# Layer ends of a two-network kernel: scaling shared by ScalarE and VectorE, weight splits behind the norm chains, transposes among the last products

## The chip, the cores and the metric

The kernel runs on one core of one Trainium2 chip. The metric is the device time of one execution in microseconds (us). The engines are named as in the profile: PE is TensorE's products (PEld its weight loads), ACT is ScalarE, DVE is VectorE, POOL is GpSimd and SP is SyncE, which issues the weight transfers.

## The reference

One sequence of 256 tokens with 1024 channels, all in float32, goes through five layers, one after another.

1. Stick-breaking attention with 16 heads: `h = h + rmsnorm(merge_heads(o) @ sb_w_o, sb_post_g)`.
2. A gated feed-forward net with a causal convolution of width 3 (`w_up` to 2 x 2816 channels, `w_down` back): `h = h + rmsnorm(f, ffn_post_g)`.
3. Forgetting attention: keys, values and gates from `rmsnorm(h, kv_norm_g) @ w_kvf`, queries from `rmsnorm(h, fox_pre_g) @ fox_w_q`, again added to h behind a norm.
4. The second feed-forward net.
5. A pooling layer (`x + y @ pool_w_out`, no norm behind it), and then a latent attention layer (`mla_*`), which starts with `rmsnorm_2(x, mla_norm) @ mla_w_in`, and a last norm.

Every layer starts with a norm of h, and every norm needs whole rows of h:

```python
def rmsnorm(x, g):
    xf = x.astype(jnp.float32)
    y = xf * lax.rsqrt(jnp.mean(xf * xf, axis=-1, keepdims=True) + RMS_EPS)
    return (y * g.astype(jnp.float32)).astype(x.dtype)
```

## The kernel before, in words

**Three products for one.** Every float32 operand x is kept as a high part (x rounded to fp32r by a copy on ACT, `hi_copy`, line 64) and a low part (x minus the high part, on DVE, `lo_sub`, line 68). A product of two such operands is three products on TensorE: high by high, high by low, low by high (`mm3`, `mm3s`). So whatever TensorE reads must first pass ACT (high) and then DVE (low).

**Weights.** All weights of the kernel form one list of chunks (1 MB each, mostly), and each chunk is cut into parts of up to 128 x 1024 elements. There are three buffers for raw chunks and eight for high and low parts (`wh`, `wl`). `bg_hi` copies the next part of the list on ACT, if the part eight places before it has been used up in the program. `bg_lo` does the DVE subtraction of every part that has its high half and not yet its low half, and, behind the last part of a chunk, issues on SP the load of the chunk three places on. `bg(m)` does m parts of both. `get_w` and `get_rows` return a function that hands out slices of a part; if the part isn't split by then, it is split at that place in the program.

**Order.** The whole program is under a manual schedule: each engine executes its instructions in the order in which the Python code emits them. An instruction that waits holds up all that were emitted behind it on its engine.

**Token blocks.** The 256 tokens are two blocks (i = 0 and 1) of 128 partitions. The residual h lies with tokens on partitions. A layer's input is the scaled h, transposed by TensorE in eight 128 x 128 squares per block (`transpose_split`: four transposes into one PSUM bank, then a high copy on ACT and a low subtraction on DVE; `all_T` does this twice, for channels 0 to 511 and 512 to 1023). [...]

**Layer ends.** `edge` (line 478) writes the end of a layer and the start of the next. `tail0` and `tail1` are the last products of blocks 0 and 1, each into two accumulators of 512 channels. `add` is either `post_add` (squares on ACT, product with the gain on DVE, rstd on POOL, then h on DVE, line 402) or, behind pooling, `plain_add` (line 409). `norm_r` squares both halves of h on ACT (line 383), does the pending weight splits (`bg_lo`) and lets POOL compute rstd (lines 346 to 349). `scaled` (line 370) multiplies h by rstd and gain, in two halves on DVE. Block 0's end runs beside block 1's last products; block 1's end runs beside the next layer's first products on block 0. Five places call `edge`: the two attentions (through `attention`, line 534), the two feed-forward nets (line 789) and pooling (line 1087).

**What follows a layer end.** Behind an attention `ffn` starts with `nat_start` (line 433): for block 0 and then block 1, two weight chunks (c) in two halves (k) give four quarters of 12 products, each with one weight part; the `hook`, which transposes block 1, stands between the blocks. Behind the second feed-forward net pooling starts with the same `nat_start`. Behind the first one `values_all` (line 452) runs over two column halves n of the value weights, and within each over the two blocks i, with hooks at given places (n, i, k). Behind pooling the latents are computed by `lat_a` (24 products with four parts) and `lat_b` (line 1129).

Of the kernel before, what the change touches and what calls it, by code (L numbers as in the profile page):

```python
# [15 lines left out]
P = 128  # L16
S = 256
NT = S // P
D = 1024
# [17 lines left out]
def tile_net(ctx: ExitStack, tc: tile.TileContext, t, out):  # L37
# [54 lines left out]
    def acc_tile(name):  # L92
        return pacc.tile([P, 512], F32, tag="acc", name=name)
# [7 lines left out]
    def tok(i):  # L101
        return slice(i * P, (i + 1) * P)
# [79 lines left out]
    def bg_lo():  # L182
        while nxt["lo"] < nxt["hi"]:
            n = nxt["lo"]
            q = parts[n]
            lo_sub(q["wl"], q.pop("raw"), q["wh"], q["scale"])
            nxt["lo"] += 1
            if n == specs[q["chunk"]][1][-1]:
                load_w(q["chunk"] + RAWB)
# [105 lines left out]
    def get_rows(idx, n=2):  # L295

        at = [get_w(i) for i in idx]
        return lambda k, c0, m: at[k // n](k % n, c0, m)
# [37 lines left out]
    def mean_sq(srcs, n):  # L336

        ss = sm.tile([P, 2], F32, tag="ss", name="ss")
        for j, x in enumerate(srcs):
            square(x, n, ss[:, j:j + 1])  # L340
        return ss[:, 0:len(srcs)]
# [29 lines left out]
                                     op0=ALU.mult, op1=ALU.mult)  # L371
        return a

    def norm_r(i):

        ss = mean_sq([h[:, i, s_] for s_ in HALF], D)
        bg_lo()
        return rstd_of(ss, "rn")

    def square(x, n, ss):  # L380

        junk = jk.tile([P, 512], BF16, tag="junk", name="junk")
# [47 lines left out]
            mm3(acc[n], at(oT, ko, tok(i)), w(kw, n * 512, 512), first and j == 0,  # L430
                last and j == len(ks) - 1)

    def nat_start(aT, views, hook):

        w = [get_w(v) for v in views]
        res = []
        for i in range(NT):
            acc = acc_tile("accS")
            for c in range(2):
                for k in range(0, KD, 4):  # L440
                    ks = range(k, k + 4)
                    mm3s(acc[:, c * 256:(c + 1) * 256], [at(aT, x, tok(i)) for x in ks],
                         [w[c](x, 0, 256) for x in ks], k == 0, k == 4)
            if i == 0:
                hook()
            x = nat.tile([P, D], F32, tag="a", name="xs")
            act.activation(out=x[:, 0:512], in_=acc, func=AF.Copy)
            res.append(x)
            bg(4)
        return res  # L450

    def values_all(xT, views, vv, hooks):


        for n in range(2):
            w = get_rows(views[n], 4)
            for i in range(NT):
                acc = acc_tile("accV")
                for k in range(0, KD, 2):
                    if (n, i, k) in hooks:  # L460
                        hooks[n, i, k]()
                    ks = range(k, k + 2)
                    mm3s(acc, [at(xT, x, tok(i)) for x in ks], [w(x, 0, 512) for x in ks],
                         k == 0, k == 6)
                    if n or i:
                        bg(1)
                if (n, i, KD) in hooks:
                    hooks[n, i, KD]()
                split(vv[0][:, i, HALF[n]], vv[1][:, i, HALF[n]], acc)
                if n == i == 0:  # L470
                    bg(2)

    def nat_T(ps, xs, c):

        for i in range(NT):
            pe.transpose(ps[:, tok(i)], xs[i][:, tok(c)], ident)

    def edge(tail0, tail1, acc, add, g, dst):


        tail0()
        half, fin = add(0, acc[0])
        half(0)
        half(1)
        bg_hi()
        fin()
        r0 = norm_r(0)
        tail1()
        half, fin = add(1, acc[1])
        half(0)  # L490
        a0 = scaled(0, r0, g)
        half(1)
        all_T(a0, dst, 0)
        bg_hi()
        fin()
        r1 = norm_r(1)
        return scaled(1, r1, g), (r0, r1)

    def attention(s0, s1, s2, s3, post, w_ids, oT, g_post, dst, hook, late, acc0_tile):

# [6 lines left out]
        for p in range(1, KD - 1):  # L507
# [6 lines left out]
            if p == 3:  # L514
# [16 lines left out]
        s3(KD - 1)  # L531
        out_rows(acc1, 1, oT, wo, K8[3:4], False, False)
        bg(1)
        return edge(lambda: out_rows(acc0, 0, oT, wo, K8[7:8], False, True),
                    lambda: out_rows(acc1, 1, oT, wo, K8[4:8], False, True, by_half=True),
                    (acc0, acc1), lambda i, a: post_add(i, a, g_post), g_next, dst)[0]

    def heads_out(p, vv, pr, oT):

# [189 lines left out]
    def ffn(l, aT, a1, late, dst):  # L729
# [3 lines left out]
        with tc.tile_pool(name=f"ff{l}", bufs=3) as ff, tc.tile_pool(name=f"fg{l}", bufs=1) as fg:  # L733
# [23 lines left out]
                split(gT[0][:, f, :], gT[1][:, f, :], y[:, 1, :])  # L757
                bg(1)

            xs = nat_start(aT, [W["up_g", l, 0], W["up_u", l, 0]], lambda: all_T(a1, aT, 1))  # L760
            for c in range(1, NF // 2):
                wg, wu = get_w(W["up_g", l, c]), get_w(W["up_u", l, c])
                for pp in range(2):
# [15 lines left out]
            for m, f in enumerate(DOWN):  # L779
# [5 lines left out]
                if m < NF - TAIL[0]:  # L785
# [1 line left out]
            tail = [[(f, f) for f in DOWN[NF - x:]] for x in TAIL]  # L787
            w = lambda f, c0, n: wd[f // 2](f % 2, c0, n)
            return edge(lambda: out_rows(acc[0], 0, gT, w, tail[0], False, True, by_half=True),
                        lambda: out_rows(acc[1], 1, gT, w, tail[1], False, True, by_half=True),  # L790
                        acc, lambda i, a: post_add(i, a, g_post), g, dst)


    def causal_mask(m):
# [43 lines left out]
    with tc.tile_pool(name="fxa", bufs=1) as fxa:  # L838
# [7 lines left out]
        with tc.tile_pool(name="fx", bufs=2) as fx, tc.tile_pool(name="fxv", bufs=1) as fxv:  # L846
# [8 lines left out]
            def scale_a(i):  # L855
                af[i] = scaled(i, rn[i], g_a)

            values_all(sT, W["fx_v"], vv, {
                (0, 0, KD): lambda: all_T(a1, sT, 1),
                (0, 1, 0): lambda: scale_a(0), (0, 1, 4): lambda: scale_a(1),  # L860
                (1, 0, 0): lambda: all_T(af[0], fT, 0),
                (1, 1, 0): lambda: all_T(af[1], fT, 1)})
            g_post = gain("fox_post_g", 0)


# [86 lines left out]
    with tc.tile_pool(name="pl", bufs=2) as pl_, tc.tile_pool(name="plc", bufs=1) as plc:  # L952
# [126 lines left out]
        def lat_mm(x, i, k0, k1):  # L1079
            n, w = lat_w[x]  # L1080
            if k0 == 0:
# [3 lines left out]
                 k0 == 0, k1 == KD)  # L1085

        a1 = edge(lambda: out_rows(acc[0], 0, st["y", 3], wo, k4, False, True, by_half=True),
                  lambda: out_rows(acc[1], 1, st["y", 3], wo, k4, False, True, by_half=True),
                  acc, plain_add, g_pre, mT)[0]
        aT = mT  # L1090


# [408 lines left out]
```

## Time and profile before

| | |
|---|---|
| median of 3 runs | 981.46 us (980.86 to 981.47) |
| profiled execution | 981.37 us, of which the span 979.7 us |
| mean granted TensorE clock | 0.999 |
| busy PE, DVE, ACT, POOL | 965.0, 756.7, 609.7, 71.9 us |
| chain that ended last | PE 88%, ACT 5%, DVE 3%, POOL 2% |

The rows that follow in the prediction are of four kinds. A timeline row has the start in us, the busy time in us, the engine, the line, the operation, the tiles written and read, their shapes, a count where like instructions are merged, and in brackets the idle time before it and the instruction that ended it. A row of a stretch has its bounds, its length, and the engine's busy time in it with the number of instructions, then the granted clock and the DMA share. A row that counts copies of weight parts ("wh<-raw") has their number since the start, the shortest, mean and longest in ns, and the first and the last start in us. The page's first row has each engine's busy time and share of the span.

### The profile page before, as it was taken

The numbers are of one execution on the slowest core, as the hardware profiler recorded it, in microseconds if no ns is written. First come the engines' busy times: TensorE is split into PE (matmuls) and PEld (weight loads), VectorE is DVE, ScalarE is ACT, GpSimd is POOL, SyncE is SP. The second block draws the span as 40 slices with busy tenths as digits, with TensorE's granted clock in tenths as the row PEclk, the third lists the DMA queues.
The fourth block names the chain that finished last, engine by engine and source line by source line (L and its number), as shares of the span: only waits on it lengthen the run. The fifth ranks groups of instructions, "written<-read, shape, count | busy, mean of one in ns | idle before, by whom it ended". The sixth has DMA issues, their size and how long they took to land.

```text
span 979.7 us, 17580 instructions
## 1 busy us (share of the span) xinstructions
PE 965.0 (99%) x6954; PEld 893.3 (91%) x6954; DVE 756.7 (77%) x1302; ACT 609.7 (62%) x1049; POOL 71.9 (7%) x181
## 2 busy tenths in 40 slices
PE   8999999999999999999999999999999999999997
PEld 6999789999888899889999988899999899999996
DVE  7577788999955969977999973776868677887876
ACT  7499866767744657666676753665434555766563
POOL 1022220000002000020000000200000020110100
PEclk9999999999999999999999999999999999999999
DMA  8724346675572744435666575375555344644521
GB/s 304 241 91 147 130 156 207 198 234 197 179 253 86 230 160 151 157 102 173 202 228 205 183 256 174 100 246 206 175 201 194 110 135 136 212 157 140 163 95 43
DMA packets 116164, 170.27 MB, mean 174 GB/s; under 512 B 4218, under 2 KB 93682, under 8 KB 116082
## 3 DMA queue, kind: packets, MB, share of 16 engines
q1 hardware_dynamic: 116002, 169.15, 51.8%
q8 instruction: 54, 0.88, 0.4%
q14 instruction: 28, 0.23, 0.1%
q0 software_dynamic: 64, 0.00, 0.0%
q10 hardware_dynamic: 16, 0.00, 0.0%
HBM read 168.10 MB, written 1.05 MB: 173 GB/s over the span
## 4 chain that ended last, share of the span: by engine, by line
PE 88%; ACT 5%; DVE 3%; POOL 2%; issue 1%; DMA 1%; SPq 0%; POOLq 0%; DVEq 0%; ACTq 0%
PE psu L79 10%; PE psu L80 10%; PE psu L81 10%; PE accD L81 4%; PE accD L80 4%; PE accD L79 4%; PE psq L79 3%; PE psq L81 3%; PE psq L80 3%; PE accO L79 2%; PE accO L81 2%; PE accO L80 2%; PE accP L79 1%; PE accP L81 1%; PE accP L80 1%; DVE wl L68 1%
## 5 line engine op out<-in xcount | busy, mean ns | idle before, releaser
L68 DVE TENSOR_TENSOR wl<-raw,wh 128x1024 fp32r<-128x1024 f32 (+3 forms) x300 | 352.6, 1197 | 88.5 <-ACT wh L64 85.5
L64 ACT ACTIVATE wh<-raw 128x1024 fp32r<-128x1024 f32 (+3 forms) x316 | 315.4, 1026 | 77.9 <-PE accD L81 30.3
L79 PE MATMUL psu<-aT,wh 128*128 128x256 f32 x864 | 239.5, 277 | 0.0
L80 PE MATMUL psu<-aT,wh 128*128 128x256 f32 x864 | 239.2, 277 | 0.0
L81 PE MATMUL psu<-aT,wl 128*128 128x256 f32 x864 | 239.2, 277 | 0.0
L79 PEld LDWEIGHTS psu<-aT,wh 128*128 128x128 f32 x864 | 162.2, 188 | 0.2
L81 PEld LDWEIGHTS psu<-aT,wl 128*128 128x128 f32 x864 | 162.2, 188 | 0.0
L80 PEld LDWEIGHTS psu<-aT,wh 128*128 128x128 f32 x864 | 162.0, 188 | 0.0
L748 DVE SCALAR_TENSOR_TENSOR yc<-psu,conv,yc 128x255 f32<-128x255 f32 (+1 forms) x160 | 73.5, 480 | 11.6 <-ACT yc L741 8.6
L79 PE MATMUL accD<-wh,gh 128*128 128x512 f32 x176 | 68.7, 390 | 0.0
L81 PE MATMUL accD<-wh,gl 128*128 128x512 f32 x176 | 68.5, 389 | 0.0
L80 PE MATMUL accD<-wl,gh 128*128 128x512 f32 x176 | 68.5, 389 | 0.0
L346 POOL TENSOR_TENSOR ss<-ss,epsc 128x1 f32<-128x1 f32 x23 | 11.6, 506 | 612.3 <-ACT junk L383 612.3
L79 PE MATMUL psq<-aT,wh 128*128 128x256 f32 x192 | 54.0, 281 | 0.1
L80 PE MATMUL psq<-aT,wh 128*128 128x256 f32 x192 | 53.4, 278 | 0.0
L81 PE MATMUL psq<-aT,wl 128*128 128x256 f32 x192 | 53.4, 278 | 0.0
L741 ACT ACTIVATE yc<-psu,conv 128x256 f32<-128x256 f32 x80 | 40.8, 560 | 19.8 <-PE psu L81 19.8
L753 ACT ACTIVATE yc<-yc 128x256 f32<-128x256 f32 x44 | 18.4, 418 | 48.5 <-DVE yc L748 48.5
L64 ACT ACTIVATE qkh<-psq 128x512 fp32r<-128x512 f32 x32 | 19.0, 594 | 33.5 <-PE psq L81 33.3
L80 PEld LDWEIGHTS accD<-wl,gh 128*128 128x128 f32 x176 | 33.1, 188 | 6.8
L79 PEld LDWEIGHTS accD<-wh,gh 128*128 128x128 f32 x176 | 33.0, 188 | 6.8
L81 PEld LDWEIGHTS accD<-wh,gl 128*128 128x128 f32 x176 | 33.0, 188 | 6.8
(347 smaller groups left out, 2272.7 us busy)
## 6 DMA issues: line engine op xcount, KB each, us to landing
raw<-in_w_up_dram SPq DMA_DIRECT2D x44, 1024.0 KB, 5.0
raw<-in_w_down_dram SPq DMA_DIRECT2D x22, 1024.0 KB, 5.9
raw<-in_pool_w_in_dram SPq DMA_DIRECT2D x16, 1024.0 KB, 7.0
raw<-in_sb_w_qkv_dram SPq DMA_DIRECT2D x10, 1024.0 KB, 5.3
raw<-in_w_kvf_dram SPq DMA_DIRECT2D x8, 1024.0 KB, 5.6
raw<-in_pool_w_out_dram SPq DMA_DIRECT2D x8, 1024.0 KB, 5.0
raw<-in_mla_w_in_dram SPq DMA_DIRECT2D x8, 1024.0 KB, 5.3
raw<-in_mla_w_out_dram SPq DMA_DIRECT2D x8, 1024.0 KB, 5.6
```

What stands on the lines that cost most here:

```text
L64: act.activation(out=hi, in_=src, func=AF.Copy, scale=scale)
L68: (eng or dve).tensor_tensor(out=lo, in0=src, in1=hi.bitcast(F32), op=ALU.subtract)
L79: pe.matmul(ps, lhsT=l[0], rhs=r[0], start=first, stop=False)
L80: pe.matmul(ps, lhsT=l[0], rhs=r[1], start=False, stop=False)
L81: pe.matmul(ps, lhsT=l[1], rhs=r[0], start=False, stop=last)
L346: pool.tensor_tensor(out=s0, in0=s0, in1=epsc[:, 0:1], op=ALU.add)
L741: act.activation(out=y[:, u, :], in_=ps[:, u * S:(u + 1) * S], func=AF.Identity, bias=cp[:, 132 + q:133 + q], scale=cp[:, 88 + q:89 + q])
L748: dve.scalar_tensor_tensor(out=y[:, u, d:S], in0=ps[:, u * S:(u + 1) * S - d], scalar=w, in1=y[:, u, d:S], op0=ALU.mult, op1=ALU.add)
L753: act.activation(out=y[:, 0, :], in_=y[:, 0, :], func=AF.Gelu_apprx_tanh)
```

## The change

- `norm_r` is gone. `norm_1` squares h, multiplies the second half of h by the gain on DVE, and computes rstd; `norm_2` multiplies that half by rstd on ACT and does the first half (h times rstd times gain) on DVE. The pending weight splits come once at the end of `edge`, and with a `tail2` also ahead of block 0's transposes.
- The feed-forward nets and pooling split block 1's last products (`halves`): all but the last step of the second accumulator ahead of block 0's transposes, that step (three products) behind them.
- The attentions have no `tail2` and lose the second `bg_hi`; the update of h stands between the two evacuations of block 0's transposes. Their `tail0` does the four products with the high half of oT first and the two with the low half last.
- In `ffn`, the hook of `nat_start` comes before the last quarter of block 0.
- `values_all` behind the first feed-forward net does block 0 for both column halves and then block 1; the hooks move accordingly.

```diff
-    def norm_r(i):
-
-        ss = mean_sq([h[:, i, s_] for s_ in HALF], D)
-        bg_lo()
-        return rstd_of(ss, "rn")
...
-    def nat_start(aT, views, hook):
+    def nat_start(aT, views, hook, early=False):
...
                 for k in range(0, KD, 4):
+                    if early and (i, c, k) == (0, 1, 4):
+                        hook()
                     ks = range(k, k + 4)
...
-            if i == 0:
+            if i == 0 and not early:
                 hook()
...
+    def values_all(xT, views, vv, hooks, order=((0, 0), (0, 1), (1, 0), (1, 1))):
+        w = [get_rows(views[n], 4) for n in range(2)]
+        for n, i in order:
+            acc = acc_tile("accV")
...
+    def norm_1(i, g):
+
+        ss = mean_sq([h[:, i, s_] for s_ in HALF], D)
+        a = nat.tile([P, D], F32, tag="a", name="a")
+        dve.tensor_tensor(out=a[:, HALF[1]], in0=h[:, i, HALF[1]], in1=g[:, HALF[1]], op=ALU.mult)
+        return a, rstd_of(ss, "rn")
+
+    def norm_2(i, a, r, g):
+
+        act.activation(out=a[:, HALF[1]], in_=a[:, HALF[1]], func=AF.Copy, scale=r)
+        dve.scalar_tensor_tensor(out=a[:, HALF[0]], in0=h[:, i, HALF[0]], scalar=r,
+                                 in1=g[:, HALF[0]], op0=ALU.mult, op1=ALU.mult)
+
+    def edge(tail0, tail1, tail2, acc, add, g, dst):
...
         fin()
-        r0 = norm_r(0)
+        a0, r0 = norm_1(0, g)
         tail1()
         half, fin = add(1, acc[1])
         half(0)
-        a0 = scaled(0, r0, g)
-        half(1)
-        all_T(a0, dst, 0)
-        bg_hi()
-        fin()
-        r1 = norm_r(1)
-        return scaled(1, r1, g), (r0, r1)
+        norm_2(0, a0, r0, g)
+        if tail2:
+            bg_lo()
+            all_T(a0, dst, 0)
+            tail2()
+            half(1)
+            bg_hi()
+            fin()
+        else:
+            half(1)
+            transpose_split(a0, dst[0], 0, 0)
+            fin()
+            transpose_split(a0, dst[1], 0, 4)
+        a1, r1 = norm_1(1, g)
+        norm_2(1, a1, r1, g)
+        bg_lo()
+        return a1, (r0, r1)
+
+    def halves(acc, i, oT, w, ks):
+        def run(n, js):
+            for j in js:
+                ko, kw = ks[j]
+                mm3(acc[n], at(oT, ko, tok(i)), w(kw, n * 512, 512), False, j == len(ks) - 1)
+
+        m = len(ks)
+        return lambda: (run(0, range(m)), run(1, range(m - 1))), lambda: run(1, [m - 1])
...
-        return edge(lambda: out_rows(acc0, 0, oT, wo, K8[7:8], False, True),
+
+        def tail0():
+            xh, xl = at(oT, KD - 1, tok(0))
+            w = [wo(KD - 1, 512 * n, 512) for n in range(2)]
+            for n in range(2):
+                for y in w[n]:
+                    pe.matmul(acc0[n], lhsT=xh, rhs=y, start=False, stop=False)
+            for n in range(2):
+                pe.matmul(acc0[n], lhsT=xl, rhs=w[n][0], start=False, stop=True)
+
+        return edge(tail0,
                     lambda: out_rows(acc1, 1, oT, wo, K8[4:8], False, True, by_half=True),
-                    (acc0, acc1), lambda i, a: post_add(i, a, g_post), g_next, dst)[0]
+                    None, (acc0, acc1), lambda i, a: post_add(i, a, g_post), g_next, dst)[0]
...
-            xs = nat_start(aT, [W["up_g", l, 0], W["up_u", l, 0]], lambda: all_T(a1, aT, 1))
+            xs = nat_start(aT, [W["up_g", l, 0], W["up_u", l, 0]], lambda: all_T(a1, aT, 1), True)
...
-                        lambda: out_rows(acc[1], 1, gT, w, tail[1], False, True, by_half=True),
-                        acc, lambda i, a: post_add(i, a, g_post), g, dst)
+                        *halves(acc[1], 1, gT, w, tail[1]), acc, lambda i, a: post_add(i, a, g_post), g, dst)
...
             values_all(sT, W["fx_v"], vv, {
-                (0, 0, KD): lambda: all_T(a1, sT, 1),
+                (1, 0, 2): lambda: all_T(a1, sT, 1),
                 (0, 1, 0): lambda: scale_a(0), (0, 1, 4): lambda: scale_a(1),
-                (1, 0, 0): lambda: all_T(af[0], fT, 0),
-                (1, 1, 0): lambda: all_T(af[1], fT, 1)})
+                (1, 1, 0): lambda: all_T(af[0], fT, 0),
+                (1, 1, 6): lambda: all_T(af[1], fT, 1)},
+                ((0, 0), (1, 0), (0, 1), (1, 1)))
...
-                  lambda: out_rows(acc[1], 1, st["y", 3], wo, k4, False, True, by_half=True),
-                  acc, plain_add, g_pre, mT)[0]
+                  *halves(acc[1], 1, st["y", 3], wo, k4), acc, plain_add, g_pre, mT)[0]
```

More of the change, by code (lines that the diff above doesn't have):

```diff
@@ L450, in nat_start @@
         return res
[L452 to L471, printed above, removed]
+    def values_all(xT, views, vv, hooks, order=((0, 0), (0, 1), (1, 0), (1, 1))):
+        w = [get_rows(views[n], 4) for n in range(2)]
+        for n, i in order:
+            acc = acc_tile("accV")
+            for k in range(0, KD, 2):
+                if (n, i, k) in hooks:
+                    hooks[n, i, k]()
+                ks = range(k, k + 2)
+                mm3s(acc, [at(xT, x, tok(i)) for x in ks], [w[n](x, 0, 512) for x in ks],
+                     k == 0, k == 6)
+                if n or i:
+                    bg(1)
+            if (n, i, KD) in hooks:
+                hooks[n, i, KD]()
+            split(vv[0][:, i, HALF[n]], vv[1][:, i, HALF[n]], acc)
+            if n == i == 0:
+                bg(2)
     def nat_T(ps, xs, c):
@@ L476, in nat_T @@
             pe.transpose(ps[:, tok(i)], xs[i][:, tok(c)], ident)
-    def edge(tail0, tail1, acc, add, g, dst):
+    def norm_1(i, g):
[8 more added lines that the diff above has]
+    def edge(tail0, tail1, tail2, acc, add, g, dst):
         tail0()
```

## The prediction, as it was put on record before the run

> **What bounds the kernel now.** I read the page first (busy shares), then TensorE's waits, then the busy time of the stretches around the five layer ends, then the order of instructions there, and last how many weight parts ScalarE had copied by given times.
>
> ```profile
> PE 965.0 (99%) x6954; PEld 893.3 (91%) x6954; DVE 756.7 (77%) x1302; ACT 609.7 (62%) x1049; POOL 71.9 (7%) x181
> ...
> 127.29:129.53 2.24, 1.43 (x10) 1.00 0.00 0
> 135.09:136.45 1.36, 1.33 (x10) 1.00 1.07 377
> 311.57:313.06 1.49, 1.04 (x10) 1.00 0.00 0
> 318.75:320.09 1.34, 1.17 (x9) 1.00 0.73 269
> 433.90:436.12 2.22, 1.41 (x9) 1.00 0.89 275
> 441.69:443.12 1.43, 1.37 (x11) 1.00 0.00 0
> 618.24:619.73 1.49, 1.04 (x10) 1.00 0.00 0
> 625.29:626.76 1.47, 1.41 (x11) 1.00 0.87 246
> 779.06:780.35 1.29, 1.04 (x9) 1.00 0.04 13
> 785.94:786.73 0.79, 0.79 (x11) 1.00 0.00 0
> ```
>
> TensorE is busy 965.0 of 979.7 us, so only its gaps can be won. Each stretch above runs from the slot after the last product ahead of a set of eight transposes to the first product behind it. The last needs 0.79 us: eight transposes that wait for nothing. The other nine take 14.33 us, 7.2 us more than nine times 0.79. That is all that layer ends can give.
>
> What the change may break is the order of DVE and ACT, which execute their instructions as written:
>
> ```profile
> L64 ACT ACTIVATE wh<-raw x39: 615/1044/1064, 6.7 to 122.7; 128x1024 fp32r<-128x1024 f32 x31, 128x512 fp32r<-128x512 f32 x8
> ...
> L64 ACT ACTIVATE wh<-raw x40: 615/1044/1064, 6.7 to 130.0; 128x1024 fp32r<-128x1024 f32 x32, 128x512 fp32r<-128x512 f32 x8
> ...
> 125.11 1.22 DVE L68 TENSOR_TENSOR wl<-raw,wh 128x1024 fp32r<-128x1024 f32 x1
> 125.42 0.95 POOL L346 TENSOR_TENSOR ss<-ss,epsc 128x1 f32<-128x1 f32 x1 [1.69 <-ACT junk L383]
> 127.31 1.42 DVE L370 SCALAR_TENSOR_TENSOR a<-h,rstd,g 128x512 f32<-128x512 f32 x2 [0.39 <-POOL rstd L349]
> 128.88 1.26 ACT L64 ACTIVATE aT<-psT 128x512 fp32r<-128x512 f32 x2 [0.45 <-PE psT L356]
> 130.78 1.40 DVE L402 SCALAR_TENSOR_TENSOR h<-y,rstd,h 128x512 f32<-128x512 f32 x2
> 132.10 1.22 DVE L68 TENSOR_TENSOR wl<-raw,wh 128x1024 fp32r<-128x1024 f32 x1
> 134.30 1.42 DVE L370 SCALAR_TENSOR_TENSOR a<-h,rstd,g 128x512 f32<-128x512 f32 x2 [0.98 <-POOL rstd L349]
> ```
>
> Counting the parts that the code defines (12 for the values, 16 for q and k, 8 for the output weights), the first part of w_up is number 37. So the copy at 122.7 is w_up part 3 of the stage that starts at 129.53, and the copy at 130.0 is part 4. That stage (nat_start) uses parts 1, 2, 3, 4 in turn, 12 products each, and 48 products fill 129.53 to 135.09: 0.116 us each. TensorE wants the low half of part 3 near 132.4 and of part 4 near 133.8. The two splits "in the chain" (125.11, 132.10) are exactly these. They aren't background work: they have a due time.
>
> **The change, part by part.** Prices: a DVE split 1.22, a DVE half with a scalar 0.71 (half of 1.42), DVE h times gain on half a row 0.65 (estimate: 0.61 is half of a split, 0.69 a half from PSUM), and ACT's scaled copy:
>
> ```profile
> 5.90 0.72 ACT L607 ACTIVATE a<-y,rstd 128x512 f32<-128x512 f32 x1 [1.68 <-POOL rstd L606]
> ...
> 120.80 0.50 PE L81 MATMUL accO<-wh,oTl 128*128 128x512 f32 x1
> ...
> 306.71 1.42 DVE L402 SCALAR_TENSOR_TENSOR h<-y,rstd,h 128x512 f32<-128x512 f32 x2 [0.27 <-POOL rstd L349]
> ...
> 310.03 1.41 DVE L370 SCALAR_TENSOR_TENSOR a<-h,rstd,g 128x512 f32<-128x512 f32 x2 [0.97 <-POOL rstd L349]
> ```
>
> *Split out of the chain.* From the start of h to the scaling takes 3.52 us with a split between (130.78 to 134.30) and 3.32 without (306.71 to 310.03). So the split costs the chain only 0.2 us, not 1.22: POOL's 0.95 us addition at 125.42 ends as the split ends (126.33). [...]
>
> *Scaling shared.* The first transposes need only the first half of a, still 0.71 us on DVE. The second half comes 0.7 us sooner from ACT, but products start on the first half's copy (128.88, 0.6 us), so at most 0.1 us is won.
>
> *Attention's last step reordered.* The high-half products go first, so accumulator 0 ends two slots later: the product at 120.80 moves to about 121.19, and its squares start 0.3 us later. The stall it avoids is 0.06 us. First restart: +0.3, -0.2, so +0.1 (129.6 to 129.7).
>
> *Two ends by attention (no tail2).* No second copy is made there, and the pending low half waits until both halves of a1 are issued. DVE's order at end 1 becomes: y to 129.75, low half of aT block 0 to 130.4, h to 131.8, low half of aT block 1 to 132.45, h times gain to 133.1, wait for rstd, a1 first half 134.0 to 134.7, then part 3's split to 135.9. TensorE stands at its second product of part 3 from about 133.1 (0.5 of it behind aT block 1) until 136.0, and finishes that quarter at 137.25. The eight transposes follow (to 138.05), placed ahead of the last quarter. Part 4 has not been copied at all: the first product that asks for it forces copy and split, behind both transposes' evacuations: ACT 137.95 to 139.1, copy to 140.15, split to 141.4. The quarter ends at 142.7, and token block 1 begins there instead of 136.45: **+6.25** (5.0 to 7.0: 0.3 either way on each of the three waits).
>
> At end 3 the same order, 306.6 us later, holds part 4 of its stage, so only the last quarter waits:
>
> ```profile
> L64 ACT ACTIVATE wh<-raw x139: 300/1047/1071, 6.7 to 429.3; 128x1024 fp32r<-128x1024 f32 x130, 128x512 fp32r<-128x512 f32 x8, 128x128 fp32r<-128x128 f32 x1
> ...
> 433.91 1.41 DVE L370 SCALAR_TENSOR_TENSOR a<-h,rstd,g 128x512 f32<-128x512 f32 x2 [0.39 <-POOL rstd L349]
> ```
>
> (135 parts precede this w_up.) The transposes, moved up 1.4 us, now wait for a1 (first half at 441.3); its split ends at 442.5; block 1 begins near 443.8 against 443.12: **+0.7** (-0.2 to 1.3).
>
> *End 2 (tail2, then the values).* Transposes ahead of the last three products hide the evacuation: restart at 312.4 instead of 313.06, -0.66. Then:
>
> ```profile
> L64 ACT ACTIVATE wh<-raw x106: 615/1047/1067, 6.7 to 313.4; 128x1024 fp32r<-128x1024 f32 x98, 128x512 fp32r<-128x512 f32 x8
> ...
> 315.68 1.22 DVE L68 TENSOR_TENSOR wl<-raw,wh 128x1024 fp32r<-128x1024 f32 x1
> ...
> 316.69 1.28 ACT L115 ACT_TABLE_LOAD   x1
> ...
> 317.59 0.40 PE L88 MATMUL accV<-wl,aT 128*128 128x512 f32 x1
> 317.88 1.55 DVE L370 SCALAR_TENSOR_TENSOR a<-h,rstd,g 128x512 f32<-128x512 f32 x2 [0.98 <-POOL rstd L349]
> ...
> 320.74 0.60 ACT L64 ACTIVATE vh<-accV 128x512 fp32r<-128x512 f32 x1
> 321.21 4.09 ACT L64 ACTIVATE wh<-raw 128x1024 fp32r<-128x1024 f32 x5
> ```
>
> Part 106 is the fourth of the values' weights (102 precede); before, its low half was ready at 316.9 for a product at 317.59. Behind a1 it comes at about 319.65, wanted at 316.85: +2.85. ACT's new scaled copy of a1 also waits for rstd, to 318.4, and the table load queued behind it ends near 319.7, still ahead of vh. The new order of values_all then takes column half 1 next, whose four parts were copied only from 321.21 on, behind vh. They still are: vh, copy (1.05), split (1.2) after block (0,0) ends leave 2.9 us of TensorE idle before (1,0); the next parts come at 1.2 us for each 1.4 us of products, 0.1 late. The wait at 318.75 (0.55 over 0.79) goes, as a1 is now wanted 7 us later. Holding all eight parts through (1,0) moves DVE's later splits back; I take 0.1 at the first q, between nothing and 0.5. Sum -0.66 + 2.85 + 2.9 + 0.1 - 0.55 + 0.1 = **+4.7** (3.0 to 5.5, each of the two long waits 0.7 shorter at best and 0.4 longer).
>
> *End 4 (tail2, pooling; its hook stays behind the quarter).* Here a0's first half comes only at 617.7, so the earlier transposes wait; restart 619.4, -0.33.
>
> ```profile
> L64 ACT ACTIVATE wh<-raw x205: 300/1047/1072, 6.7 to 620.0; 128x1024 fp32r<-128x1024 f32 x98, 128x512 fp32r<-128x512 f32 x4, 128x128 fp32r<-128x128 f32 x1
> ...
> 624.54 1.42 DVE L370 SCALAR_TENSOR_TENSOR a<-h,rstd,g 128x512 f32<-128x512 f32 x2 [0.98 <-POOL rstd L349]
> ```
>
> 201 parts precede, so part 205 is the fourth quarter's, wanted at 623.6. The scaling keeps its time (+0.1); one half to 625.35, split to 626.6: 3.0 us late. **+2.6** (1.8 to 3.3).
>
> *End 5 (tail2, latents).* Restart 779.87, -0.48.
>
> ```profile
> 781.71 1.16 DVE L68 TENSOR_TENSOR wl<-raw,wh 128x960 fp32r<-128x960 f32 x1
> ...
> 784.17 1.55 DVE L370 SCALAR_TENSOR_TENSOR a<-h,rstd,g 128x512 f32<-128x512 f32 x2 [1.30 <-POOL rstd L349]
> ```
>
> This split serves the product after the 24 first ones, now at 784.2; behind a1 (near 784.4) it ends at 785.55: 1.3 late. **+0.9** (0 to 1.4; later waits for DVE could absorb it).
>
> Each late split also issues SP's next weight load later, by up to 10 us; such a load brings a chunk three ahead of the one in use, so I count nothing, and nothing else is moved past SP or POOL.
>
> Sum: 6.25 + 4.7 + 0.7 + 2.6 + 0.9 = 15.15. The profiled execution took 981.37 us (span 979.7), 0.1 below the median 981.46. Forecast 981.4 + 15.1 = **996.5 us**; bounds 991.0 (981.4 and the lows, 9.6) to 999.9 (the highs, 18.5).
>
> **Rivals.** *Faster:* the pending splits are not what TensorE wants next (if my part numbers are off by two or more), and the evacuations are hidden in the seven places beside the two restarts after attention. These two cost 1.45 and 1.43 of the 7.2, set by rstd, scaling, transposes and evacuation; the rest, 4.3 us, goes: 977.1. It decides as soon as the splits cost less than 2.3 us. Against it: five counts that all land on the next stage's parts. *No change:* that, but with the moved-up transposes waiting for a1 at ends 1 and 3 and only 1 to 2 us won: 980. *Clock:* idle stretches near 3 us let TensorE's clock fall.
>
> ```profile
> 1.43 1.76 PE L583 MATMUL warm<-ident 128*128 128x128 f32 x7 [1.43 <-POOL ident L326]
> ```
>
> At the start seven transposes take 1.76 us, 0.25 each against 0.1 later, and such rates last to about 5.5 us. Half speed for 4.1 us costs 2 us; behind four stalls of 2.8 to 3.1 us that is 8: 1004.5. No gap behind the start in this trace exceeds 1 us, so nothing here decides it. [...]
>
> **How the numbers follow.** A measurement tells about 0.2% (2 us) from nothing. Forecast 0.74, clock 0.13, faster 0.06, no change 0.07. So slower 0.87, same 0.07, faster 0.06. The forecast's own range is 991 to 999.9; to hold 8 in 10 it reaches up to the clock case and two below for terms that overlap: 989 to 1004.5.
>
> **What would show it.** New waits of TensorE for wl (L68's low halves) of 2.8 to 3.1 us at the new places of 133.1, 316.9, 623.6 and for wh and wl at the values' second block and the last quarter of end 1; waits for aT gone at ends 2, 4, 5. The chain of waits should run through DVE's wl there. If instead wl ends before a1's scaling in DVE's order, or the count of copies at 122.7 belongs to other weights, the sum is wrong; a first product behind a stall at 0.2 us for 256 columns would show the clock.

## The result, and the profile after

The changed kernel takes 1004.89 us (median; 1003.48 to 1010.3), the kernel before 981.16 us beside it: 1.0252 times as long, 95% interval 1.0214 to 1.0290. The forecast was 996.5 us with 1004.5 as its upper end. The profiled execution of the changed kernel took 1005.41 us (span 1003.7).

The page's first part and its row of the granted clock (tenths of full speed in 40 slices):

```profile
PE 975.1 (97%) x6954; PEld 903.4 (90%) x6954; DVE 756.7 (75%) x1302; ACT 616.6 (61%) x1059; POOL 71.1 (7%) x181
...
PEclk9999989999999799999999999999999999999999
```

TensorE runs the same 6954 instructions. The span grew by 24.0 us. Of these 13.9 are idle time (979.7 - 965.0 = 14.7 before, 1003.7 - 975.1 = 28.6 now), and 10.1 are busy time: the same products took longer. The forecast had 15.15 of the first and nothing of the second.

The idle part is where it was looked for. TensorE's waits (who waits, for what; us in total, times, longest):

```profile
PE accS L88 <- DVE wl L68: 6.1, 3, 2.9
PE accV L88 <- DVE wl L68: 3.6, 3, 2.8
...
PE accS L87 <- ACT wh L64: 1.7, 1, 1.7
PE accV L87 <- ACT wh L64: 1.6, 1, 1.6
...
PE accL L88 <- DVE wl L68: 1.1, 1, 1.1
PE psu L79 <- ACT zs L1002: 1.1, 1, 1.1
```

The low halves of weights (wl) and two high halves (wh) that come late now end the waits. (The last row, for a tile of pooling, is 0.9 us in the runs of the shared scaling alone and of the moved hook alone too.) In the kernel before, TensorE's two longest waits for low halves of weights are these, in the latent attention and in the first layer's values, and it has none at the ends:

```profile
PE psq L81 <- DVE wl L68: 0.5, 1, 0.5
...
PE accV L88 <- DVE wl L68: 0.3, 1, 0.3
```

The order of instructions at end 1, with the idle time ahead of each in brackets:

```profile
133.78 0.75 DVE L483 SCALAR_TENSOR_TENSOR a<-h,rstd,g 128x512 f32<-128x512 f32 x1 [0.72 <-POOL rstd L349]
134.45 1.22 DVE L68 TENSOR_TENSOR wl<-raw,wh 128x1024 fp32r<-128x1024 f32 x1
135.72 0.58 PE L88 MATMUL accS<-wl,aT 128*128 128x256 f32 x1 [2.35 <-DVE wl L68]
136.10 0.42 PE L87 MATMUL accS<-wh,aT 128*128 128x256 f32 x1
136.32 0.41 PE L88 MATMUL accS<-wl,aT 128*128 128x256 f32 x1
...
141.24 0.39 PE L87 MATMUL accS<-wh,aT 128*128 128x256 f32 x1 [1.68 <-ACT wh L64]
142.50 0.58 PE L88 MATMUL accS<-wl,aT 128*128 128x256 f32 x1 [0.87 <-DVE wl L68]
```

The split of part 3 stands behind a1's first half, and TensorE stands until 135.72; part 4 gives two waits more. But then look at the next rows: products of 256 columns start 0.22 us apart (136.10, 136.32), where 0.116 was the rate in this stage before. That is the busy time that grew. The same rows by stretches of 3.41 us, the columns being the stretch, its length, PE's busy time, the granted clock, the DMA share and GB/s:

```profile
131.99:135.40 3.41, 1.30 (x9) 1.00 0.00 0
135.40:138.81 3.41, 3.09 (x14) 0.50 0.00 0
138.81:142.23 3.42, 1.14 (x8) 1.00 0.00 0
142.23:145.64 3.41, 3.14 (x14) 0.50 0.59 181
329.95:333.37 3.42, 0.61 (x3) 1.00 0.01 2
333.37:336.78 3.41, 2.03 (x5) 0.50 0.64 145
336.78:340.20 3.42, 2.71 (x6) 0.50 0.07 28
340.20:343.61 3.41, 3.41 (x14) 0.50 0.91 298
643.99:647.40 3.41, 0.56 (x5) 1.00 0.01 0
647.40:650.81 3.41, 3.41 (x17) 0.50 0.67 198
```

In this trace the clock is 1.00 or 0.50 for whole stretches of 3.41 us, on one grid. Each of the four falls comes behind a stretch in which TensorE was busy for 0.56 to 1.30 of 3.41 us, and each return behind one in which it was busy for 3.09 to 3.41 us. At end 2 this takes three stretches, since the waits that end at 337.03 (1.63 us, for wh) and 338.29 (0.46) leave the first two of them busy for 2.03 and 2.71 us alone. The executions without a trace lost clock too: the four of the changed kernel have a mean granted clock of 0.983 to 0.990, those of the kernel before 0.998 to 0.999.

The rest of the longer busy time has a second cause, which no wait shows. First and last start of the products of the first feed-forward net, of before and then of the changed kernel, in a stretch at full clock without a wait:

```profile
L79 PE MATMUL psu<-aT,wh x306: 276/276/278, 142.0 to 245.7; 128*128 128x256 f32 x153
...
L79 PE MATMUL psu<-aT,wh x309: 280/280/283, 151.0 to 259.8; 128*128 128x256 f32 x155
```

With the two other products of each three, that is 0.113 us a product before (103.7 us over 3 x 305) and 0.1177 now (108.8 over 3 x 308). Nothing in the change touches them. One net has 960 such products, so the slower pace costs about 4.3 us. Both paces turn up in the profile of before too (0.1133 us in the nets, 0.1178 in most of pooling), and its executions spread by this step: of seven beside the first experiments three took 980.5 to 981.0 us and three 985.3 to 985.4. In the table below net 1 is slow in the changed kernel and fast in the same kernel with fillers. So I take this term as a draw and not as an effect of the change.

For the comparison of kernels I cut each profile at the same products of TensorE and take the differences to the profile of before (us). End 1 runs from the last product of the attention's heads to the feed-forward net's first step, end 2 from the first product of accD to the first of the gates behind the values, and so on; "nets" are the steps of the two feed-forward nets, "rest" is the start, the second attention and all behind end 5. The rows behind the first are the experiments that follow.

| kernel | end 1 | net 1 | end 2 | end 3 | net 2 | end 4 | pooling | end 5 | rest | all |
|---|---|---|---|---|---|---|---|---|---|---|
| changed kernel | 8.63 | 4.26 | 8.12 | 0.15 | 0.00 | 3.47 | -1.22 | 0.89 | -0.28 | 24.02 |
| spin | 5.60 | 0.00 | 4.95 | 0.13 | 0.00 | 1.97 | -0.40 | 0.89 | 0.04 | 13.18 |
| split_late | 5.85 | 4.26 | 2.92 | 3.91 | 0.00 | 5.22 | -0.20 | 2.21 | -0.29 | 23.88 |
| split_back | 2.07 | 4.26 | 5.48 | 2.07 | 4.28 | 0.23 | 0.00 | 0.06 | -0.11 | 18.34 |
| old_order | 7.16 | 0.00 | 2.34 | 0.37 | 4.27 | 1.97 | 0.45 | 0.92 | 0.18 | 17.66 |
| halves_only | 0.19 | 4.27 | 0.30 | -0.02 | 0.01 | 0.39 | -0.12 | -0.50 | -0.47 | 4.05 |
| shared_only | 2.28 | 0.00 | 0.94 | 1.32 | 4.27 | 0.20 | 0.83 | 0.38 | -0.37 | 9.85 |
| early_only | 1.07 | 0.00 | 0.00 | 1.31 | 4.27 | -0.17 | 0.74 | 0.00 | -0.11 | 7.11 |

### The profile page after: what moved, and what is told of

The parts are those of the page before. It is cut to its first block, busy times and chain, and to the rows that moved or that the text cites. A ratio compares the mean times of both kernels' runs of the same rounds, so it can differ in the third digit from the quotient of the medians.

```text
span 1003.7 us, 17582 instructions
## 1 busy us (share of the span) xinstructions
PE 975.1 (97%) x6954; PEld 903.4 (90%) x6954; DVE 756.7 (75%) x1302; ACT 616.6 (61%) x1059; POOL 71.1 (7%) x181
## 4 chain that ended last, share of the span: by engine, by line
PE 84%; ACT 7%; DVE 4%; POOL 2%; issue 1%; DMA 1%; POOLq 0%; SPq 0%; DVEq 0%; ACTq 0%
PE psu L79 10%; PE psu L81 10%; PE psu L80 10%; PE accD L80 4%; PE accD L79 4%; PE accD L81 4%; PE psq L79 3%; PE psq L81 3%; PE psq L80 3%; PE accO L79 2%; DVE wl L68 2%; PE accO L81 2%; PE accO L80 2%; ACT wh L64 2%; PE accV L88 2%; PE accP L79 1%
## 5 line engine op out<-in xcount | busy, mean ns | idle before, releaser
L346 POOL TENSOR_TENSOR ss<-ss,epsc 128x1 f32<-128x1 f32 x23 | 10.1, 440 | 627.6 <-ACT junk L377 627.6
```

Source lines behind the costliest of these rows:

```text
L346: pool.tensor_tensor(out=s0, in0=s0, in1=epsc[:, 0:1], op=ALU.add)
```

## The experiments

My theory after the result had three terms: the waits for late splits (about 13.5 us), halved clock behind them (about 8), and the pace of the nets (a draw). Its rivals were that the splits are innocent and other parts of the change cost the time, and that the slow products come from something other than the gaps ahead of them.

**split_late: the late splits alone.** The kernel before, with the pending low halves behind block 1's scaling:

```diff
         ss = mean_sq([h[:, i, s_] for s_ in HALF], D)
-        bg_lo()
         return rstd_of(ss, "rn")
...
-        return scaled(1, r1, g), (r0, r1)
+        a1 = scaled(1, r1, g)
+        bg_lo()
+        return a1, (r0, r1)
```

> The kernel before with one edit alone: the two weight splits leave the norm chains and are done once, behind block 1's scaling. Theory (a split has a due time, set by the next stage's products): new waits of TensorE for wl of about 4.2 us at end 1, 3 us at ends 2, 3 and 4, 2 us at end 5, so 15 us from waits, and up to 7 us more if the clock falls behind four of them: 996 to 1005 us, point 1001. Rival (the loss of the changed kernel comes from its new places for transposes and scaling, the splits are background work): at most 983 us, perhaps 1 us faster than before, since each chain loses 0.2 us of POOL's wait.

Measured: 1002.74 us (999.65 to 1007.93), ratio 1.0202 (1.0155 to 1.0248). This one edit gives most of the loss. In its waits, which by ends are 4.0, 2.7, 2.7, 2.7 and 1.9 us for the 4.2, 3, 3, 3 and 2 of the theory:

```profile
PE accS L88 <- DVE wl L68: 9.5, 3, 4.0
PE accV L88 <- DVE wl L68: 3.0, 2, 2.7
PE accL L88 <- DVE wl L68: 1.9, 1, 1.9
```

The clock fell three times (at 137.88, 455.32 and 643.05). It doesn't follow that the other parts are free; the next two runs show that they are not, and that the parts don't add up.

**split_back: all but the late splits.** The changed kernel with the splits in the norm chains again, and the second copy in the two ends behind attention:

```diff
         dve.tensor_tensor(out=a[:, HALF[1]], in0=h[:, i, HALF[1]], ...)
+        bg_lo()
         return a, rstd_of(ss, "rn")
...
             transpose_split(a0, dst[0], 0, 0)
+            bg_hi()
             fin()
```

> The changed kernel with the splits put back into the norm chains (behind the new product on DVE), and the second copy of a part back in the attentions; all else as changed. Theory (due times): waits for wl at ends 1, 4 and 5 go. Left are the moved-up transposes waiting for a1 (+0.6 at ends 1 and 3), the gains at ends 2, 4 and 5 (-1.2, -0.3, -0.5) and the second value block's wait for its weights (+2.9, with 0 to 3.4 of lost clock): 983 to 987 us. Rival (transposes and scaling are at fault): stays at 995 us or more. If the slower pace of the first feed-forward net's products (0.1177 instead of 0.1133 us) comes from the fallen clock, it is 0.1133 here.

Measured: 993.54 us (989.78 to 999.72), ratio 1.0109 (1.0058 to 1.0160): a good half of the loss is gone, but it lies 6.5 us above the expected range. In its profile both nets ran at the slower pace (8.5 us). The clock had not fallen ahead of net 1 here (its first fall is at 329.40), so that net's pace doesn't come from a fallen clock. The rest is in the waits:

```profile
PE psT L356 <- DVE a L484: 4.2, 3, 1.7
PE accV L87 <- ACT wh L64: 2.9, 1, 2.9
```

The first are two waits of 1.67 us on block 0's transposes at the ends 1 and 3 (0.76 before; the run of the shared scaling alone, below, has 1.23 of each and shows the cause of that much) and one of 0.82 us on block 1's, moved up at end 1. The second is the values' new order, which asks for parts that ACT has not yet copied. The clock fell behind it (to 0.50 at 329.40), and behind the wait at end 3 (at 448.87).

**old_order: the values' order alone undone.** The changed kernel with the blocks of `values_all` in the order of before:

```diff
-                (1, 0, 2): lambda: all_T(a1, sT, 1),
+                (0, 0, KD): lambda: all_T(a1, sT, 1),
...
-                (1, 1, 0): lambda: all_T(af[0], fT, 0),
-                (1, 1, 6): lambda: all_T(af[1], fT, 1)},
-                ((0, 0), (1, 0), (0, 1), (1, 1)))
+                (1, 0, 0): lambda: all_T(af[0], fT, 0),
+                (1, 1, 0): lambda: all_T(af[1], fT, 1)})
```

> The changed kernel with the old order of the value blocks and its hooks. Theory (due times): only the wait of the second value block goes (2.1 us of waits in the changed kernel's trace, and some of the half-speed products around it): 3 to 6 us off, 999 to 1002 us. Rival (that wait is covered or comes back elsewhere): no change, 1004 us.

Measured: 999.0 us (998.77 to 1001.37), ratio 1.0165 (1.0130 to 1.0201), as expected. End 2 costs 2.34 instead of 8.12 us. Its wait of 2.8 us for wl is still there, but here two stretches of the grid share it, busy for 0.63 and 0.55 of their length, and the clock stayed. The ends 1 and 4 have the same waits as the changed kernel, to 0.1 us, and only one fall of the clock instead of three (end 1: 7.16 against 8.63, end 4: 1.97 against 3.47). So between these two kernels the same waits differ by about 1.5 us of clock at each of these ends, by where they lay on the grid. This varies from one execution to the next: the profiled one of this kernel has a mean granted clock of 0.997, the other three 0.988 to 0.992.

**spin: the same waits without idle stretches.** The changed kernel with 20 to 24 spare transposes of the identity ahead of the five longest waits; they use what is there, and nothing uses them:

```diff
+    def spin(n):
+        ps = mm_tile("warm")
+        for _ in range(n):
+            pe.transpose(ps[:, 0:P], ident, ident)
```

> The changed kernel with 20 to 24 spare transposes on TensorE ahead of each of the five products that wait longest (two at end 1, two at end 2, one at end 4), about 2.2 us each, written to a PSUM tile that nobody reads. Theory (the clock halves when TensorE has done too little in a stretch of 3.41 us): waits stay as long, granted clock stays at 1.00, about 8 us come back: 995 to 998 us, near the forecast without the clock, 996.5. Rival (half speed has another cause than idleness): 1003 us or more, and the granted clock falls as before.

Measured: 997.1 us (992.41 to 1004.61), ratio 1.0146 (1.0089 to 1.0204) where the changed kernel has 1.0252, although TensorE has 108 instructions more. The granted clock of its profile has no fall ahead of the program's last 3 us, in which every profile here has one (0.5 for its last 1.3 to 3.0 us), and it is 0.998 to 0.999 in all four executions. (They still spread over 12 us. The pace of the two nets can give 8.5 of it; the rest is open.) What is left of the waits, and one of the fillers:

```profile
PE accS L88 <- DVE wl L68: 1.0, 3, 0.6
...
133.28 2.35 PE L430 MATMUL warm<-ident 128*128 128x128 f32 x20
135.90 0.39 PE L88 MATMUL accS<-wl,aT 128*128 128x256 f32 x1 [0.15 <-DVE wl L68]
```

The product at end 1 starts at 135.90, not sooner than in the changed kernel (135.72): the wait is still paid, only the clock isn't. Behind each of the five fillers a wait of 0.15 to 0.64 us is left, so none of them held up a product for long. So the ends of this run are the price of the waits alone: 5.60 + 4.95 + 0.13 + 1.97 + 0.89 = 13.5 us. The differences of the changed kernel to it, 3.0 at end 1, 3.2 at end 2 and 1.5 at end 4, are the clock: 7.7 us in the profiled execution.

**stalls: how long must a gap be?** The kernel before, with a stall behind every second step of both nets: a transpose, a chain of small ACT copies that reads it, and a transpose of what the last of them wrote.

```diff
+                    if pp == 1 and f < 20:
+                        st = ff.tile([P, P], F32, tag="st", name="st")
+                        pe.transpose(spare[:, 0:P], ident, ident)
+                        junk = jk.tile([P, 512], BF16, tag="junk", name="junk")
+                        for _ in range((f - 1) // 2 + (l % 2)):
+                            act.activation(out=junk[:, 0:P], in_=spare[:, 0:P], func=AF.Copy)
+                        act.activation(out=st, in_=spare[:, 0:P], func=AF.Copy)
+                        pe.transpose(spare[:, 0:P], st, ident)
                     conv_gate(f, ps)
```

> The kernel before with nine stalls put in each of its two feed-forward nets, one after every second step's products: TensorE waits for a chain of 2 to 10 (first net) or 3 to 11 (second net) copies of 128x128 on ScalarE, so for about 1 to 4 us, growing. Theory (the granted clock is set anew every 3.41 us; it halves behind a window in which TensorE was busy for less than about 0.4 of it, and comes back behind a window that was nearly full): stalls under 1.7 us never halve the clock, stalls of 2.1 to 3.2 us do so or not, by where they lie in the grid of windows, and those above 3.3 us nearly all do; each halved window begins on one common grid of 3.41 us. Rival (a window must be wholly idle): no halving below 3.4 us. A second rival (the length of the stall alone decides, not the grid): one length above which each stall halves the clock, at a fixed distance behind its start.

Measured: one execution of 1036.54 us, 18 stalls, the longest 3.32 us, and four falls, all on one grid. Four of the stalls, with their length in brackets, then the stretch of the grid that each of them lies in, and the one behind it where the clock fell:

```profile
232.69 0.33 PE L776 MATMUL spare<-ident,st 128*128 128x128 f32 x1 [2.39 <-ACT st L775]
536.55 0.33 PE L776 MATMUL spare<-ident,st 128*128 128x128 f32 x1 [2.08 <-ACT st L775]
566.68 0.33 PE L776 MATMUL spare<-ident,st 128*128 128x128 f32 x1 [2.70 <-ACT st L775]
597.62 0.33 PE L776 MATMUL spare<-ident,st 128*128 128x128 f32 x1 [3.32 <-ACT st L775]
...
230.45:233.86 3.41, 1.17 (x10) 1.00 0.95 305
233.86:237.27 3.41, 3.41 (x18) 0.50 0.00 1
534.23:537.65 3.42, 1.34 (x12) 1.00 0.80 251
537.65:541.06 3.41, 3.41 (x18) 0.50 1.00 357
564.95:568.36 3.41, 1.68 (x15) 1.00 0.77 268
595.67:599.09 3.42, 1.47 (x13) 1.00 0.57 234
599.09:602.50 3.41, 3.41 (x18) 0.50 0.00 0
...
261.17:264.58 3.41, 1.57 (x13) 1.00 0.71 276
578.61:582.02 3.41, 1.00 (x9) 1.00 0.74 287
```

Behind a stall of 2.08 us, which lay within one stretch (busy 1.34 us of 3.42, 0.39), the clock halved; behind one of 2.70 us, which began before its stretch (busy 1.68 us, 0.49), it did not. The last two rows hold the ends of two stalls of the same length, 3.01 us (at 263.01 and 581.02): the first left its stretch busy for 0.46, and the clock stayed; the second for 0.29, and it fell. The two of 2.08 and the two of 2.39 us are divided in the same way. So both rivals fall: none of the stretches ahead of the four falls was wholly idle (busy for 0.29 to 0.43), and no single length of the stall decides. The theory stands in this run; the one exception, in another, is noted below.

**halves_only: transposes among the last products, alone.** The kernel before with `tail2` and `halves` at the ends 2, 4 and 5 (their code as in the change).

```diff
-        half(1)
-        all_T(a0, dst, 0)
+        if tail2:
+            all_T(a0, dst, 0)
+            tail2()
+            half(1)
+        else:
+            half(1)
+            all_T(a0, dst, 0)
```

> The kernel before with one part of the change: at the ends 2, 4 and 5 block 1's last product stands behind block 0's transposes. Theory (what was gained at block 0's restart is given back at block 1's transposes, since block 1's chain sets them): against the profile of before, the stretches end 2 (accD to psf), end 4 (accD to psu) and end 5 (psg to psz) change by -0.5 to +0.1 us each, about -0.5 in all. Rival (each restart is worth its own shift): -0.6 at each, -1.5 in all. Neither expects a stretch in which the granted clock is halved. The total may differ by a further 4.3 us for each feed-forward net whose products run at the other of the two paces, which says nothing on this.

Measured: 982.79 us (981.32 to 987.17), ratio 1.0021 (1.0002 to 1.0040), with net 1 at the slower pace in the profile. The three ends give +0.30, +0.39 and -0.50, 0.2 in all: the rival's -1.5 is not there, and the theory's -0.5 is off by 0.7. Only end 5 keeps the gain. At end 2 block 0's restart comes 0.37 us sooner, and block 1's transposes cost 0.54 more; at end 4 it is 0.10 and 0.27, with 0.39 more in the products between.

**shared_only: the shared scaling alone,** with the splits where they were:

```diff
         ss = mean_sq([h[:, i, s_] for s_ in HALF], D)
+        a = nat.tile([P, D], F32, tag="a", name="a")
+        dve.tensor_tensor(out=a[:, HALF[1]], in0=h[:, i, HALF[1]], in1=g[:, HALF[1]], op=ALU.mult)
         bg_lo()
```

> The kernel before with one part of the change: the scaling of a block shared by VectorE and ScalarE, the weight splits where they were. Theory: the transposes of the first half still stand behind VectorE's work on that half, and the extra product of h and the gain on VectorE takes up what ScalarE takes off: each of the five ends -0.3 to +0.3 us, in all within 1 us of before. Rival (the sharing shortens each chain by VectorE's second half, 0.66 us): -0.7 at each end, -3.5 in all. No halved clock by either.

Measured: 985.35 us (983.71 to 991.22), ratio 1.0051 (1.0032 to 1.0070). Both expectations are missed: the ends 1, 2 and 3 are longer by 2.28, 0.94 and 1.32 us. Block 1's norm at end 3 shows how:

```profile
440.97 1.41 DVE L410 SCALAR_TENSOR_TENSOR h<-y,rstd,h 128x512 f32<-128x512 f32 x2
...
442.41 0.69 DVE L378 TENSOR_TENSOR a<-h,g 128x512 f32<-128x512 f32 x1
...
443.02 1.22 DVE L68 TENSOR_TENSOR wl<-raw,wh 128x1024 fp32r<-128x1024 f32 x1
443.43 0.86 POOL L348 TENSOR_TENSOR ss<-ss 128x1 f32<-128x1 f32 x1 [0.28 <-ACT junk L391]
...
444.95 0.75 DVE L385 SCALAR_TENSOR_TENSOR a<-h,rstd,g 128x512 f32<-128x512 f32 x1 [0.71 <-POOL rstd L349]
```

The split now starts 0.7 us later and runs beside POOL's second addition, which ends at 444.29, next to the split's end (444.24), and takes 0.86 instead of 0.19 us. From h to the scaling it is 3.98 us (440.97 to 444.95), against 3.52 before. Block 0's norm at the ends 1 and 3 has the same order, and its transposes wait 1.23 us there for 0.76 before. Of end 3's 1.32 us block 0's restart gives 0.66 and block 1's 0.30; slower products give the rest. So with the split where it was the shared scaling costs time, and taking the split out is what costs the waits. At end 1 the clock also fell once behind the longer gap (0.50 from 130.84 to 134.25).

**early_only: the moved hook alone.** The kernel before with block 1's transposes ahead of the last quarter at the ends 1 and 3:

```diff
+                    if early and (i, c, k) == (0, 1, 4):
+                        hook()
...
-            if i == 0:
+            if i == 0 and not early:
                 hook()
```

> The kernel before with one part of the change: at the ends 1 and 3 block 1's transposes stand one quarter earlier among the products of the feed-forward net's first step. Theory (block 1's scaled rows are not there yet, as in the run with the splits put back, where the same quarter gave a wait of up to 2.1 us on each of these ends): +0.6 to +2.0 us at each of the ends 1 and 3, nothing elsewhere; +1.2 to +4 in all, and more only if a window of the clock falls behind one of these waits. Rival (the transposes come earlier and the products of block 1 with them): -0.5 at each.

Measured: 985.52 us (983.13 to 988.50), ratio 1.0039 (1.0021 to 1.0057). End 1 is longer by 1.07 and end 3 by 1.31 us, as the theory said (though the run that it leaned on had only 0.82 us from this at end 1, the rest being block 0's); net 2's slower pace makes up most of the rest. The wait at end 1:

```profile
135.64 1.32 PE L356 MATMUL psT<-ident,a 128*128 128x128 f32 x8 [1.22 <-DVE a L370]
```

**breaks: the two paces.** The kernel before with 1 to 4 spare transposes ahead of each step of both nets:

```diff
+                    for _ in range(1 + f % 4):
+                        pe.transpose(spare[:, 0:P], ident, ident)
```

> The kernel before with 1 to 4 spare transposes (3, 4, 1, 2, 3, 4, 1, ...) ahead of each of the 20 steps of products in both feed-forward nets; no wait is added, and their results are not used. First theory (the pace of back-to-back 256-column products is drawn anew at each break, by nothing but chance): a mixture of steps at 0.1134 and at 0.1178 us within each net, with no pattern in the number of transposes. Second theory (the break's own length sets the pace): all steps behind the same number of transposes run at one pace. Third (a break without a wait leaves the pace as it is): one pace through each net, as in the kernel before. 40 breaks with 2.5 transposes in the mean cost about 0.2 to 0.4 us each, 8 to 16 us in all, and the two paces shift that by at most 8.6.

Measured: one execution of 1002.31 us, 18.7 above the kernel before beside it, as expected for breaks and paces together. In both nets the second step ran at 0.1134 us a product and the other 19 at 0.1178. The second and the third step of net 1, by the first and last start of one of each three products:

```profile
L80 PE MATMUL psu<-aT,wh x16: 276/276/276, 149.4 to 154.5; 128*128 128x256 f32 x16
...
L80 PE MATMUL psu<-aT,wh x16: 280/280/282, 155.0 to 160.3; 128*128 128x256 f32 x16
```

The third theory falls, since the pace changed at breaks without a wait. So does the second: five steps of each net stand behind four transposes, and one of the five is fast. The first doesn't fit well either, as it is the same step in both nets. In the kernel with stalls the full stretches of 3.41 us count 33 products behind some stalls and 31 behind others (33 from 179.25, 31 from 192.90, 33 from 206.55, 31 from 220.21), with no pattern that I saw. So in the run with breaks the pace (0.1134 or 0.1178 us) was kept through each step and changed at breaks alone; what settles it stays open.

Two parts of the change have no run of their own: the new order in the attentions' last step, and the place of the update of h there.

## Why the prediction was wrong

*The sum of the waits was right to 1.6 us.* Against the waits alone (the spin row of the table): end 1 6.25 predicted, 5.60 measured; end 2 4.7 and 4.95; end 3 0.7 and 0.13; end 4 2.6 and 1.97; end 5 0.9 and 0.89; 15.15 and 13.5 in all. The order on DVE at end 1 came out nearly to the tenth: a1's first half at 133.78 for 134.0, the split to 135.67 for 135.9, TensorE free at 135.72 for 136.0. The part numbers counted from the code were right: all long new waits are for the parts named. The reading that the splits in the chains have a due time is shown by the first experiment.

*The step that failed is the one that put the clock at nothing.* It stood in the prediction as the rival Clock alone. The prediction said that "no gap behind the start in this trace exceeds 1 us, so nothing here decides it", gave it 0.13, and let the forecast stand without it, with 1004.5 as the range's upper end alone. That the clock would cost nothing was my estimate, which no row of that trace showed. The trace of before could indeed not decide it: its one fall, at 978.05, comes behind a stretch without any product, past the last one. But then the case should have had a chance nearer to a half, as four of the predicted stalls were of 2.8 to 3.1 us. The runs put 7.7 us in the place of nothing: two falls at end 1, a long one at end 2, one at end 4, with a stall of 2.35 us enough for the first. The rival gave 1004.5, and 1004.89 came; that its total is so near is in part luck. In the profiled execution the waits were 1.6 us shorter than it counted, the clock cost 7.7 us for its 8 (taken from slow transposes at the program's start, from 1.43 to 5.50 us, where the granted clock of the trace of before is 1.00), and the paces of nets and pooling, which it didn't have, added 3.0. Of the 15 falls in six kernels 14 came behind a stretch of the grid that was busy for 0.15 to 0.43 of its length, and the fifteenth behind one busy for 0.52.

*What was not in the prediction at all is the pace of the nets:* 4.26 us in net 1 of the profiled execution, given back in part in pooling (-1.22, in spite of a wait of 1.1 us for zs there). By the profiles it moves a time by steps of 4.3 us, and is why the times of the small experiments say less than their table rows.

*Smaller points.* The split was priced at 0.2 us of the chain; from h to the scaling the changed kernel takes 3.32 us at end 1 (130.46 to 133.78) for 3.52 before: the 0.2 that the rows gave, and it went into the waits behind it. In block 0's norm there POOL's addition at 125.98 took 0.55 us and ended at 126.53, next to the end of the new product of h and gain at 126.47; in block 1's the addition at 132.10, ahead of the product, took 0.19. The wait at end 3 that was to cost 0.7 isn't there: a1 comes 3.9 us behind block 0's restart for 4.8 before, so block 1's transposes find its first half all but ready. The gains at the restarts of ends 2 and 4 came (about 0.6 us each for 0.66 and 0.33), but with the splits in place end 2's is given back at block 1's transposes and end 4's hardly arises, as the run with the halves alone shows.

## What to carry to other kernels

An operation that looks like background work in a critical chain may have a due time of its own: count which piece of the stream it is, and when TensorE asks for it, before moving it. Price a stall of TensorE not by its length alone: in these runs stalls of 2.1 to 3.0 us halved the clock or not, depending on where they lay, and a fall cost 1.5 us where it lasted one stretch (end 4) and 3.2 where it lasted three (end 2); some 20 spare transposes in each long gap bought that back. When parts of a change are judged apart, look at the stretches of the trace and not at the total alone, where another effect moves the total by more.

## What the runs showed of the hardware that was not expected

In the six kernels with a fall ahead of the program's end the granted clock was 1.00 or 0.50 for whole windows of 3.41 us, on one grid in each trace (in the kernel with stalls one grid fits four falls, spread over 365 us, to a tenth). In these six every window at full clock that was busy for 0.43 or less (the program's start and its last 10 us aside) was followed by half clock, and of those between 0.45 and 0.62 all but one stayed at full. The exception:

```profile
127.43:130.84 3.41, 1.77 (x13) 1.00 0.00 0
130.84:134.25 3.41, 3.41 (x18) 0.50 0.03 7
```

This window of the kernel with the shared scaling alone was busy for 0.52, of which eight transposes took 1.08 us. Behind a window with little but transposes the clock stayed at full: in the run with fillers the one from 137.32 to 140.73 was busy for 3.33 us, nearly all of it with 28 transposes. Whether they count for less than products was not tried. At half clock the windows busy for 0.59, 0.79 and 0.82 were followed by another at half, and those of 0.83 to 1.00 by full clock.

In the two nets, products of 256 columns ran at 0.1134 or 0.1178 us each at the same granted clock of 1.00 and without a wait; in the run with breaks the pace held from one break to the next, and it is worth 4.3 us in a net of 960 products.
